# Two zero columns between prompt and sample tokens, and a pool of its own for the split-y ring, in a four-layer diffusion backbone

## The chip, the cores and the metric

One core of one Trainium2 chip. The metric is the device time of one execution in microseconds. TensorE is called PE below, its weight loads PEld, VectorE DVE, ScalarE ACT, GpSimd POOL and SyncE SP. L340 is line 340 of the kernel before.

## The reference

One inference step of a hybrid backbone, in float32: 128 prompt tokens and 256 sample tokens, D = 1024, four layers. Layers 0 and 3 mix tokens with a bidirectional Mamba-2 scan (SSD), layer 1 with a short gated convolution, layer 2 with differential attention. Each layer is followed by an FFN with a depthwise convolution. Around every sub-layer stand an RMS norm, and a shift, a scale and a gate that are computed from the condition with `w_mod`.

```python
def dwconv(x, w):                      # per group: prompt and sample each padded with zeros
    out = xp[:, 0:L] * w[0]
    for i in range(1, k):              # k = 3
        out = out + xp[:, i:i + L] * w[i]

def conv_ffn(h, w_up, conv_w, w_down):
    u = dwconv(h @ w_up, conv_w)
    gate, val = jnp.split(u, 2, axis=-1)
    return (jax.nn.silu(gate) * val) @ w_down

def ssd_mixer(...):
    z, xbc, dt_raw = jnp.split(h @ w_in, ...)
    xbc = jax.nn.silu(dwconv(xbc, conv_w) + conv_b)
    ...                                # scan forwards and backwards in chunks of 128 tokens
    y = rmsnorm(y * jax.nn.silu(z), norm_g)
    return y @ w_out
```

## The kernel before, in words

All 384 tokens (one tile of 128 prompt tokens, two tiles of sample tokens) go through the layers together. The normed and modulated activations h lie channel-major: hh and hl, eight blocks of 128 channels by T = 384 tokens, are two float32r parts whose sum is h. Weights are loaded in chunks of 128x1024 (`ahead`, L143), split in two float32r parts on ACT (L155) and DVE (L156), four chunks ahead of their use.

**Channel-major products** (`cm_block`, L331): for each block of 128 output channels PE runs 8 x 3 matmuls (hi hh, hi hl, lo hh) of 128x384 into one PSUM bank (L340). The FFN has 44 such blocks in a layer, an SSD layer 6 in each of its 8 groups, the short convolution 24.

**Convolutions** (`conv`, L393): ACT copies the block out of PSUM times the middle tap (L396). DVE then adds the left and the right neighbour, for the prompt's 128 columns and the samples' 256 apart, since the two groups must not mix: four instructions of 127 and 255 columns (L398, L400). Their last one lets the PSUM bank go. The products have five banks in the FFN and three (mm) beside two (yp) in an SSD layer.

**The SSD layer** (`ssd` L508, `ssd_core` L611): a loop over 8 groups. The scan of group g (`scan`, L645) is written in five steps, between which the products of group g + 1 are written (L754 to L758). `decay(t)` (L674) builds the weights of a token tile on POOL (L678, L679), DVE (L682, L686, L687, L693) and ACT; `out(t)` (L717) multiplies them into the two yp banks (L722), three tiles side by side in 384 columns. L741 reads both banks to the end and writes y. `gated` (L634) multiplies with the gate (L637), squares on ACT (L642) and sums on POOL (L643). In the last group no further products are written beside the scan except the gate's.

Memory: y, ssq and the ring of split y (yh, yl, seven each, `prep` L528) belong to the pool `mix`, which is open for the whole layer. The pool `core` holds dt, nine slots c (convolved blocks and squares), acs, wdt and dec, and above it the pool `scan` holds ab, st, xt, cb and others. When they close, their memory goes to the pool `out` of the output stage. These pools have `reuse_waits="tile"`: a tile waits for the tiles that lay in its memory.

**The output stage** (`_tm_out`, L359): token-major products of 128x512, two halves, k outermost: nine matmuls for each k (L380), with `prep(k)` splitting y[k] on ACT (L532) and DVE (L533) at most three k ahead as written. In the FFN L405 and L406 do this for fg.

The order of the instructions on each engine is made by the framework's scheduler from a simulated timeline, not by the order as written: an instruction that is ready early can be placed early, and each engine then works in that fixed order. Modulation (L187, 1 MB of `w_mod` for each unit) is written between the products by `pace` (L242).

Of the kernel before, what the change touches and what calls it, by code (L numbers as in the profile page):

```python
# [19 lines left out]
P = 128  # L20
D = 1024
KB = D // P
T = 384
# [9 lines left out]
TOK = [(0, 128), (128, 128), (256, 128)]  # L33
# [11 lines left out]
class Net:  # L45
# [22 lines left out]
    @contextmanager  # L68
    def banked(self, **banks):
        """Five banks of PSUM, by what they are for."""  # L70
        with self.tc.tile_pool(name="ps", bufs=1, space=PSUM, reuse_waits="tile") as ps:
            self.ps, self.banks = ps, banks
            yield
# [46 lines left out]
    def plan(self, l):  # L120
        """The chunks of weights that layer l multiplies with, in their order."""
# [21 lines left out]
    def ahead(self):  # L143
        """Start the loads and the splits of the next chunks."""
# [22 lines left out]
    def mod_units(self, l):  # L167
        """Closures that compute layer l's modulation; a unit is a megabyte of w_mod."""
# [56 lines left out]
    def modbuf(self):  # L225
        """A buffer for a unit of w_mod: the standing ones, or one of those that a phase has room for."""
# [15 lines left out]
    def pace(self, phase, n, of):  # L242
        """Modulation beside the products of a phase, n parts of which are done."""
# [22 lines left out]
    def rstd(self, sa, sb, eps=EPS):  # L266
        """(sa + sb + eps) ** -0.5"""
# [11 lines left out]
    def normed(self, t, ss):  # L279
        """The rows of token tile t, normed."""  # L280
# [7 lines left out]
    def turned(self, xn, banks=0):  # L288
        """Channel-major: two banks of [128 channels, 4 blocks, 128 tokens]."""
# [8 lines left out]
    def modulated(self, l, which, t, trs):  # L298
        """h's columns of token tile t, in two float32r parts."""
# [14 lines left out]
    def gated(self, t, hf, acc, gt, parts):  # L314
        """Half a token tile of m: its squares' sum and its product with the gate."""
# [5 lines left out]
    def residual(self, t, parts, eps=EPS):  # L321
        """x += gate * rmsnorm(m) * g for token tile t; the new rows' sums of squares."""
# [8 lines left out]
    def cm_block(self, chunks, nblk, b, m=P, tag="mm"):  # L331
        """[m channels, tokens] of h @ W; chunks: (first kb, number, hi, lo) as [128, kb, nblk, m]."""
# [18 lines left out]
    def tm_out(self, *args, room, **kw):  # L351
        """m = g @ W token-major, both halves, then the residual of each token tile."""
# [40 lines left out]
    def conv(self, src, cw):  # L393
        """Depthwise convolution of three taps along the tokens of both groups."""
        t = self.cpool.tile([P, T], F32, tag="c", name="cv", bufs=self.cbufs)
        self.S.activation(t, src, AF.Copy, scale=cw[:, 1:2])  # L396
        for o, n in ((0, 128), (128, 256)):
            self.V.scalar_tensor_tensor(t[:, o + 1:o + n], src[:, o:o + n - 1], cw[:, 0:1], t[:, o + 1:o + n],  # L398
                                        op0=ALU.mult, op1=ALU.add)
            self.V.scalar_tensor_tensor(t[:, o:o + n - 1], src[:, o + 1:o + n], cw[:, 2:3], t[:, o:o + n - 1],  # L400
                                        op0=ALU.mult, op1=ALU.add)
# [7 lines left out]
    def run(self):  # L409
# [24 lines left out]
        for n, l in enumerate(self.layers):  # L434
# [4 lines left out]
            def norm(t, ss, l, which):  # L439
                if t == 0:  # L440
                    self.new_h()
# [66 lines left out]
    def ssd(self, l, pl, then):  # L508
# [11 lines left out]
        # eps over the square of the rows' norm factor, which is left out of y  # L520
        sp = self.pt.tile([P, 512], F32, tag="tp", name="sps")
        for t in range(NT):
            PE.matmul(sp[:, t:t + 1], ssq[:, t * P:(t + 1) * P], self.ones1, start=True, stop=True)
# [4 lines left out]
        def prep(k):  # L528
            hi = pl.tile([P, T], F32R, tag="yh", name="yh", bufs=RB)
            lo = pl.tile([P, T], F32R, tag="yl", name="yl", bufs=RB)  # L530
            g = dn[:, k // 2, k % 2, 1:2]
            S.activation(hi, y[k], AF.Copy, scale=g)  # L532
            V.scalar_tensor_tensor(lo, y[k], g, hi.bitcast(F32), op0=ALU.mult, op1=ALU.subtract)  # L533
            return hi, lo

        self.tm_out(l, 0, 16, prep, eps=eps, then=then, room=1)

    def steps(self, j, keep, pl, between):
        """Time steps and decays: dt, the cumulated a*dt (token-major, and by rows in DRAM), and what states need."""
# [10 lines left out]
        for t in range(NT):  # L550
            PE.transpose(tr[:, t, :64], raw[:, t * P:(t + 1) * P], self.ident[:64, :64])
# [8 lines left out]
        # log1p(u) = 2 atanh(z), z = u / (2 + u) <= 1/3  # L560
# [17 lines left out]
        # cumulated within a chunk, forwards and backwards: rows of heads  # L578
        rows = pl.tile([64, T], F32, name="rows")
# [440 lines left out]
```

## Time and profile before

| | |
|---|---|
| median of 3 runs | 2426.16 us (2422.03 to 2428.34) |
| the profiled execution: span of core 0 | 2425.7 us (no time of its own outside the span is listed) |
| instructions | 35610 |
| mean granted clock of PE | 0.974 of 2.4 GHz |
| PE, DVE, ACT, POOL busy | 2298.7, 1647.8, 1225.8, 378.5 us |

Stages of the span: SSD layer 0 from about 60 to 455 us (scan groups up to 380), its FFN to 755; the short convolution to 870, with its output stage and norms to 925, its FFN to 1200; attention to 1460, its FFN to 1755; SSD layer 3 to 2140 (groups up to 2071), its FFN to the end. Busy times of PE count a matmul from its start to its modelled end, and matmuls overlap, so the start-to-start time of neighbours is the pace, not the duration of one.

### The profile page before, as it was taken

What the parts mean: (1) busy time and instruction counts of PE and PEld (TensorE: products, weight loads), DVE (VectorE), ACT (ScalarE), POOL (GpSimd) and SP (SyncE); (2) the same over time, 40 slices, a digit from 0 to 9 for tenths busy, and PEclk for the clock granted to TensorE, in tenths of its full rate; (3) what the DMA queues carried; (4) which work ended last, traced back from release to release, by engine and by line L of the source; (5) the groups of instructions that cost most, each with busy time, mean ns of one, the idle gap of its engine ahead of it and who ended that gap; (6) DMA issues with size and microseconds to landing.
All of it is one profiled execution on the core that took longest, in us unless ns stands there. A gap on an engine that the chain in (4) does not pass through costs nothing.

```text
span 2425.7 us, 35610 instructions
## 1 busy us (share of the span) xinstructions
PE 2298.7 (95%) x13132; PEld 2007.5 (83%) x13132; DVE 1647.8 (68%) x2926; ACT 1225.8 (51%) x2031; POOL 378.5 (16%) x546
## 2 busy tenths in 40 slices
PE   6889999899999999999999989999998999989998
PEld 3778887599987978998688758998687888779987
DVE  3789877487755447776654547776669988677765
ACT  3646656454444344444544444445555766554444
POOL 1133330100001001000123330000114344010000
PEclk7989999999999999999999989999999999989999
DMA  7556565543547564335435453345455655423342
GB/s 285 173 164 194 171 202 191 200 137 122 165 120 268 212 215 162 130 122 165 148 116 178 164 205 128 123 131 163 138 171 174 194 160 162 133 97 122 126 146 85
DMA packets 113374, 391.79 MB, mean 162 GB/s; under 512 B 13104, under 2 KB 25520, under 8 KB 100912
## 3 DMA queue, kind: packets, MB, share of 16 engines
q1 hardware_dynamic: 113200, 389.52, 49.1%
q8 instruction: 103, 1.69, 0.3%
q14 instruction: 71, 0.58, 0.1%
HBM read 382.39 MB, written 7.08 MB: 161 GB/s over the span
## 4 chain that ended last, share of the span: by engine, by line
PE 76%; DVE 8%; DMA 3%; issue 2%; ACT 2%; POOL 2%; SPq 0%; POOLq 0%; DVEq 0%; ACTq 0%
PE mm L340 42%; PE mm L380 20%; PE mm L807 5%; PE modps L187 2%; PE yp L380 2%; DVE w L686 2%; DVE e L682 1%; DVE wl L156 1%; PE yp L848 1%; PE yp L722 1%; DMA wm<-in_w_mod 1%; DMA h<-in_state 1%; ACT jk L263 1%; DVE w L687 1%; POOL r L273 1%
## 5 line engine op out<-in xcount | busy, mean ns | idle before, releaser
L340 PE MATMUL mm<-hh,wh 128*128 128x384 f32 (+1 forms) x2352 | 798.0, 341 | 19.1 <-DVE cv L400 13.6
L340 PE MATMUL mm<-hl,wh 128*128 128x384 f32 (+1 forms) x2352 | 796.1, 339 | 0.0
L340 PE MATMUL mm<-hh,wl 128*128 128x384 f32 (+1 forms) x2352 | 792.1, 338 | 0.0
L156 DVE TENSOR_TENSOR wl<-wr,wh 128x1024 fp32r<-128x1024 f32 (+2 forms) x466 | 565.3, 1215 | 262.9 <-ACT wh L155 261.1
L155 ACT ACTIVATE wh<-wr 128x1024 fp32r<-128x1024 f32 (+2 forms) x466 | 483.2, 1039 | 328.0 <-PE mm L340 265.0
L340 PEld LDWEIGHTS mm<-hh,wh 128*128 128x128 f32 (+1 forms) x2352 | 444.3, 189 | 45.6 <-DVE cv L400 20.4
L340 PEld LDWEIGHTS mm<-hl,wh 128*128 128x128 f32 (+1 forms) x2352 | 443.9, 189 | 6.5 <-issue 4.2
L340 PEld LDWEIGHTS mm<-hh,wl 128*128 128x128 f32 (+1 forms) x2352 | 443.6, 189 | 2.6 <-issue 0.7
L396 ACT ACTIVATE cv<-mm,fcw 128x384 f32<-128x384 f32 x176 | 100.1, 571 | 233.2 <-PE mm L340 228.2
L380 PE MATMUL mm<-wh,gh 128*128 128x512 f32 x528 | 208.7, 395 | 0.0
L380 PE MATMUL mm<-wl,gh 128*128 128x512 f32 x528 | 208.6, 395 | 0.0
L380 PE MATMUL mm<-wh,gl 128*128 128x512 f32 x528 | 207.9, 395 | 0.0
L271 POOL TENSOR_SCALAR m<-s 128x1 f32<-128x1 f32 x42 | 17.6, 419 | 1146.7 <-ACT jk L263 1145.8
L398 DVE SCALAR_TENSOR_TENSOR cv<-mm,fcw,cv 128x127 f32<-128x127 f32 x352 | 144.1, 410 | 42.6 <-ACT cv L396 42.6
L405 ACT ACTIVATE gh<-fg 128x384 fp32r<-128x384 f32 x176 | 92.2, 524 | 152.6 <-PE mm L380 151.7
L406 DVE TENSOR_TENSOR gl<-fg,gh 128x384 fp32r<-128x384 f32 x176 | 97.6, 557 | 96.7 <-ACT gh L405 96.0
L400 DVE SCALAR_TENSOR_TENSOR cv<-mm,fcw,cv 128x127 f32<-128x127 f32 x352 | 145.8, 415 | 10.8
L380 PEld LDWEIGHTS mm<-wh,gh 128*128 128x128 f32 x528 | 99.0, 187 | 24.9 <-issue 0.8
L380 PEld LDWEIGHTS mm<-wh,gl 128*128 128x128 f32 x528 | 99.0, 187 | 24.3
L380 PEld LDWEIGHTS mm<-wl,gh 128*128 128x128 f32 x528 | 99.0, 187 | 23.9
L686 DVE SCALAR_TENSOR_TENSOR w<-cb,dt,w 128x128 f32<-128x128 f32 x192 | 94.8, 550 | 3.2 <-POOL w L679 3.2
L187 PE MATMUL modps<-wm,sil 128*32 128x512 f32 x496 | 81.8, 658 | 14.1 <-DMA wm<-in_w_mod 13.2
(223 smaller groups left out, 3206.2 us busy)
## 6 DMA issues: line engine op xcount, KB each, us to landing
wr<-in_ffn_up SPq DMA_DIRECT2D x176, 512.0 KB
wm<-in_w_mod SPq DMA_DIRECT2D x62, 1024.0 KB
wr<-in_ssd_in SPq DMA_DIRECT2D x96, 512.0 KB
wr<-in_ffn_down SPq DMA_DIRECT2D x88, 512.0 KB
wx<-in_w_mod SPq DMA_DIRECT2D x34, 1024.0 KB
ab<-acs SPq DMA_DIRECT2D x48, 512.0 KB
wr<-in_ssd_out SPq DMA_DIRECT2D x32, 512.0 KB
wr<-in_sc_in SPq DMA_DIRECT2D x32, 384.0 KB
```

Source lines behind the costliest of these rows:

```text
L155: self.S.activation(hi[:, :m], raw[:, :m], AF.Copy)
L156: self.V.tensor_tensor(lo[:, :m], raw[:, :m], hi[:, :m].bitcast(F32), op=ALU.subtract)
L187: self.PE.matmul(acc[32 * j:32 * j + 32, :], self.sil[:, kb, :], raws[:, j // 2, (j % 2) * 512:(j % 2 + 1) * 512], start=kb == 0, stop=kb ...
L340: self.PE.matmul(acc[:m], w, h, start=n == 0, stop=n == len(ops) - 1)
L380: self.PE.matmul(acc[t], g[:, o:o + n], w, start=k == 0 and i == 0, stop=k == nk - 1 and i == 2)
L396: self.S.activation(t, src, AF.Copy, scale=cw[:, 1:2])
L398: self.V.scalar_tensor_tensor(t[:, o + 1:o + n], src[:, o:o + n - 1], cw[:, 0:1], t[:, o + 1:o + n], op0=ALU.mult, op1=ALU.add)
L400: self.V.scalar_tensor_tensor(t[:, o:o + n - 1], src[:, o + 1:o + n], cw[:, 2:3], t[:, o:o + n - 1], op0=ALU.mult, op1=ALU.add)
L405: self.S.activation(hi, src, AF.Copy)
L406: self.V.tensor_sub(lo, src, hi.bitcast(F32))
L686: V.scalar_tensor_tensor(w[:, sl], cb[:, 0, t, :], dt[:, t, hs:hs + 1], w[:, sl], op0=ALU.mult, op1=ALU.add)
L807: PE.matmul(acc[t][:, :256], h[k][:, o:o + m], w[:, ws], start=k == 0 and i == 0, stop=k == KB - 1 and i == 2)
```

## The change

h gets two zero columns between prompt and samples: T is 386, and the token tiles lie at 0, 130 and 258. hh and hl are made once, their gap is set to zero once, and later layers write the three tiles again; `norm` no longer makes new ones. Every tile with T columns is two columns wider, and every channel-major product yields zeros in the gap, so a convolution is two sums of 385 columns over the whole row. In the scan the gap of each yp bank is set to zero on DVE before L722 writes the tiles, as L741 reads all T columns. Slices `t * P:(t + 1) * P` of such tiles become `TS[t]`. The ring of split y moves from the pool `mix` to a pool `yhl`, opened after `core` has closed.

```diff
-T = 384
+GAP = 2
+T = 384 + GAP
-TOK = [(0, 128), (128, 128), (256, 128)]
+TOK = [(0, 128), (128 + GAP, 128), (256 + GAP, 128)]
+TS = [slice(o, o + m) for o, m in TOK]
...
     def new_h(self):
         hh = [self.hp.tile([P, 4, T], F32R, name=f"hh{i}") for i in range(2)]
         hl = [self.hp.tile([P, 4, T], F32R, name=f"hl{i}") for i in range(2)]
+        for a in hh + hl:
+            self.V.memset(a[:, :, P:P + GAP].bitcast(F32), 0.0)
...
     def conv(self, src, cw):
         t = self.cpool.tile([P, T], F32, tag="c", name="cv", bufs=self.cbufs)
         self.S.activation(t, src, AF.Copy, scale=cw[:, 1:2])
-        for o, n in ((0, 128), (128, 256)):
-            self.V.scalar_tensor_tensor(t[:, o + 1:o + n], src[:, o:o + n - 1], cw[:, 0:1], t[:, o + 1:o + n],
-                                        op0=ALU.mult, op1=ALU.add)
-            self.V.scalar_tensor_tensor(t[:, o:o + n - 1], src[:, o + 1:o + n], cw[:, 2:3], t[:, o:o + n - 1],
-                                        op0=ALU.mult, op1=ALU.add)
+        self.V.scalar_tensor_tensor(t[:, 1:], src[:, :T - 1], cw[:, 0:1], t[:, 1:], op0=ALU.mult, op1=ALU.add)
+        self.V.scalar_tensor_tensor(t[:, :T - 1], src[:, 1:], cw[:, 2:3], t[:, :T - 1], op0=ALU.mult, op1=ALU.add)
         return t
...
             def norm(t, ss, l, which):
-                if t == 0:
-                    self.new_h()
...
-        def prep(k):
-            hi = pl.tile([P, T], F32R, tag="yh", name="yh", bufs=RB)
-            lo = pl.tile([P, T], F32R, tag="yl", name="yl", bufs=RB)
...
-        self.tm_out(l, 0, 16, prep, eps=eps, then=then, room=1)
+        with self.tc.tile_pool(name=f"yhl{l}", bufs=1, reuse_waits="tile") as yp:
+            def prep(k):
+                hi = yp.tile([P, T], F32R, tag="yh", name="yh", bufs=RB)
+                lo = yp.tile([P, T], F32R, tag="yl", name="yl", bufs=RB)
...
+            self.tm_out(l, 0, 16, prep, eps=eps, then=then, room=1)
...
             mv1 = decay(1)
             yp = [self.psum("yp") for _ in range(2)]
+            for b in range(2):
+                V.memset(yp[b][:, P:P + GAP], 0.0)
             out(0, mv0)
```

## Rows read from the trace of the kernel before

**Rows 1.** The page, part 1: busy time of each engine.
```profile
PE 2298.7 (95%) x13132; PEld 2007.5 (83%) x13132; DVE 1647.8 (68%) x2926; ACT 1225.8 (51%) x2031; POOL 378.5 (16%) x546
```

**Rows 2.** Busy times by stage: window and its length, engines, granted clock, DMA share, GB/s.
```profile
125.00:367.00 242.00, 225.80 (x1471) 198.00 (x1472) 204.82 (x385) 146.47 (x206) 90.33 (x93) 0.96 0.58 183
...
925.00:1108.00 183.00, 183.00 (x1057) 182.92 (x1057) 134.35 (x248) 80.31 (x115) 0.00 (x0) 1.00 0.39 124
...
1850.00:2060.00 210.00, 204.09 (x1381) 185.36 (x1380) 189.79 (x359) 143.06 (x201) 88.25 (x85) 1.00 0.57 172
```
The five engines stand in the order PE, PEld, DVE, ACT, POOL.

**Rows 3.** Waits, whole run: us in total, times, longest us.
```profile
PE mm L340 <- DVE cv L400: 13.6, 14, 2.4
...
PE yp L722 <- DVE w L687: 13.4, 8, 4.6
```

**Rows 4.** The page's group of L340, and PE's timeline: start us, us, engine, line, operation.
```profile
L340 PE MATMUL mm<-hh,wh 128*128 128x384 f32 (+1 forms) x2352 | 798.0, 341 | 19.1 <-DVE cv L400 13.6
...
362.59 0.39 PE L380 MATMUL mm<-wl,yh 128*128 128x512 f32 x1
...
364.93 0.40 PE L380 MATMUL mm<-wh,yl 128*128 128x512 f32 x1
...
559.84 0.33 PE L340 MATMUL mm<-hh,wh 128*128 128x384 f32 x1
...
562.96 0.33 PE L340 MATMUL mm<-hh,wh 128*128 128x384 f32 x1
```

**Rows 5.** Timeline of DVE in the scan core of layer 3, at 1998.
```profile
1997.89 0.34 DVE L400 SCALAR_TENSOR_TENSOR cv<-mm,cw,cv 128x127 f32<-128x127 f32 x1
1998.15 0.47 DVE L398 SCALAR_TENSOR_TENSOR cv<-mm,cw,cv 128x255 f32<-128x255 f32 x1
1998.55 0.33 DVE L682 SCALAR_TENSOR_TENSOR e<-ab,acs,e 128x128 f32<-128x128 f32 x1
```

**Rows 6.** Groups by line, DVE, each form apart: a memset.
```profile
L103 DVE MEMSET ones<- 128x1 f32 x1 | 0.1, 59 | 0.0
```

**Rows 7.** ACT's busy time on L532 alone, windows in layers 0 and 3.
```profile
125.00:350.00 225.00, 4.23 (x7) 0.96 0.58 185
1830.00:1940.00 110.00, 4.23 (x7) 0.98 0.64 190
```

**Rows 8.** Timeline of DVE and POOL, end of the scan in layers 0 and 3.
```profile
377.79 1.13 DVE L741 SCALAR_TENSOR_TENSOR y<-cv,dn,yp 128x384 f32<-128x384 f32 x2
...
2069.88 1.13 DVE L741 SCALAR_TENSOR_TENSOR y<-cv,dn,yp 128x384 f32<-128x384 f32 x2
...
380.02 3.26 POOL L643 TENSOR_TENSOR ssq<-ssq,sq 128x384 f32<-128x384 f32 x2 [12.29 <-ACT sq L642]
...
2072.11 2.54 POOL L643 TENSOR_TENSOR ssq<-ssq,sq 128x384 f32<-128x384 f32 x2 [10.19 <-ACT sq L642]
```

**Rows 9.** PE and PEld on L380 alone, from the tail's start to four moments.
```profile
355.00:376.90 21.90, 9.60 (x38) 6.87 (x39) 1.00 0.46 157
355.00:382.00 27.00, 14.70 (x59) 10.98 (x60) 1.00 0.53 181
2050.00:2068.90 18.90, 11.91 (x44) 7.99 (x45) 1.00 0.27 73
2050.00:2073.00 23.00, 16.01 (x61) 11.31 (x62) 1.00 0.36 102
```

**Rows 10.** DVE on L533 alone, in both tails, up to L741.
```profile
355.00:377.70 22.70, 2.36 (x4) 1.00 0.47 157
2050.00:2069.80 19.80, 2.35 (x4) 1.00 0.28 76
```

**Rows 11.** Busy times and granted clock at the turn of layer 3, columns as in rows 2.
```profile
2130.00:2150.00 20.00, 11.55 (x53) 10.51 (x54) 13.12 (x23) 10.53 (x26) 5.79 (x8) 0.66 0.20 68
```

**Rows 12.** Timeline of DVE: end of decay(0) and of decay(1) in one group.
```profile
1985.25 0.68 DVE L687 TENSOR_TENSOR w<-w,e 128x512 f32<-128x512 f32 x1
...
1990.22 0.68 DVE L687 TENSOR_TENSOR w<-w,e 128x512 f32<-128x512 f32 x1
```

More of the change, by code (lines that the diff above doesn't have):

```diff
@@ L522, in ssd @@
         for t in range(NT):
-            PE.matmul(sp[:, t:t + 1], ssq[:, t * P:(t + 1) * P], self.ones1, start=True, stop=True)
+            PE.matmul(sp[:, t:t + 1], ssq[:, TS[t]], self.ones1, start=True, stop=True)
         ep = pl.tile([P, NT], F32, name="ep")
@@ L526, in ssd @@
         eps = [ep[:, t:t + 1] for t in range(NT)]
-        def prep(k):
-            hi = pl.tile([P, T], F32R, tag="yh", name="yh", bufs=RB)
-            lo = pl.tile([P, T], F32R, tag="yl", name="yl", bufs=RB)
[L531 to L534, printed above, removed]
-        self.tm_out(l, 0, 16, prep, eps=eps, then=then, room=1)
+        with self.tc.tile_pool(name=f"yhl{l}", bufs=1, reuse_waits="tile") as yp:
+            def prep(k):
+                hi = yp.tile([P, T], F32R, tag="yh", name="yh", bufs=RB)
+                lo = yp.tile([P, T], F32R, tag="yl", name="yl", bufs=RB)
+                g = dn[:, k // 2, k % 2, 1:2]
+                S.activation(hi, y[k], AF.Copy, scale=g)
+                V.scalar_tensor_tensor(lo, y[k], g, hi.bitcast(F32), op0=ALU.mult, op1=ALU.subtract)
+                return hi, lo
+            self.tm_out(l, 0, 16, prep, eps=eps, then=then, room=1)
     def steps(self, j, keep, pl, between):
@@ L550, in steps @@
         for t in range(NT):
-            PE.transpose(tr[:, t, :64], raw[:, t * P:(t + 1) * P], self.ident[:64, :64])
+            PE.transpose(tr[:, t, :64], raw[:, TS[t]], self.ident[:64, :64])
         dt = keep.tile([P, NT, 64], F32, name="dt")
@@ L577, in steps @@
         between()
-        rows = pl.tile([64, T], F32, name="rows")
+        rows = pl.tile([64, NT * P], F32, name="rows")
         for dr, tri in ((0, self.Ur), (1, self.Lr)):
@@ L584, in steps @@
                     PE.matmul(ps[:64, t * P:(t + 1) * P], a[:, t, :], tri, start=n == 0, stop=n == 1)
-            V.tensor_copy(rows[32 * dr:32 * dr + 32], ps[32 * dr:32 * dr + 32, :T])
+            V.tensor_copy(rows[32 * dr:32 * dr + 32], ps[32 * dr:32 * dr + 32, :NT * P])
         gd = self.dp.tile([NT, 2, 32, P], F32, name=f"acs{j}")
@@ L662, in scan @@
                 for t in range(NT):
-                    PE.transpose(tr[:, t, :], src[:, t * P:(t + 1) * P], self.ident)
+                    PE.transpose(tr[:, t, :], src[:, TS[t]], self.ident)
                 S.activation(dst, tr[:, 0:3, :], AF.Copy)
@@ L666, in scan @@
             for t in range(NT):
-                PE.matmul(cbp[:, t, :], Bc[:, t * P:(t + 1) * P], Cc[:, t * P:(t + 1) * P], start=True, stop=True)
+                PE.matmul(cbp[:, t, :], Bc[:, TS[t]], Cc[:, TS[t]], start=True, stop=True)
             cb = pl.tile([P, 2, NT, P], F32, tag="cb", name="cb")
@@ L692, in decay @@
                     c3 = ce.rearrange("p r (h q) -> p (r h) q", h=4)
-                    V.tensor_tensor(c3, c3, Cc[:, None, t * P:(t + 1) * P].to_broadcast([P, 8, P]), op=ALU.mult)
+                    V.tensor_tensor(c3, c3, Cc[:, None, TS[t]].to_broadcast([P, 8, P]), op=ALU.mult)
                     mv += [(hst[t, dr], ce[:, dr]) for dr in range(2)]
@@ L721, in out @@
                             hh = 2 * b + i
-                            PE.matmul(yp[b][64 * i:64 * i + 64, t * P:(t + 1) * P], a[:, hh * HP:(hh + 1) * HP],
+                            PE.matmul(yp[b][64 * i:64 * i + 64, TS[t]], a[:, hh * HP:(hh + 1) * HP],
                                       m[:, hh * P:(hh + 1) * P], start=n == 0, stop=n == len(mv) - 1, tile_position=(0, 64 * i))
@@ L789, in proj @@
         def proj(n, out):
-            qT = pl.tile([P, 2, T], F32, tag="qT", name="qT", bufs=2)
+            qT = pl.tile([P, 2, NT * P], F32, tag="qT", name="qT", bufs=2)
             kT = pl.tile([P, 2, 4 * P], F32, tag="kT", name="kT", bufs=2)
@@ L882, in heads @@
                     PE.transpose(tr[:, dh, :], on[:, dh, :], self.ident)
-                hi, lo = [a[n][:, :, t * P:(t + 1) * P] for a in (oh, ol)]
+                hi, lo = [a[n][:, :, TS[t]] for a in (oh, ol)]
                 S.activation(hi, tr[:, 0:2, :], AF.Copy, scale=gs)
```

## The prediction

> **What bounds the kernel now.** I read the page first: TensorE (PE) is busy 95% of the 2425.7 us span [rows 1]. Then the busy times by stage. In an FFN's up-projection (925 to 1108) PE is busy all of 183 us, while VectorE (DVE) has a quarter of its time to spare. In the scan cores of the two SSD layers (125 to 367, 1850 to 2060) DVE is busy 85% and 90%, and PE, with gaps, 93% and 97% [rows 2]. So a DVE instruction saved under an FFN buys nothing, one saved in an SSD core may. The table of waits gives the ceiling for that: in the whole run PE waited 13.6 us for a convolution to release its PSUM bank (L340 behind L400) and 13.4 us for the scan's weights (L722 behind L687) [rows 3], 27.0 us together.
>
> The queries by line and the timeline then settle the two prices that pull the other way: the pitch of the products, and what the ring of split y does today.
>
> **Two more columns in every channel-major product.** 3 x 2352 matmuls on L340 get 386 columns in place of 384. Their rows show 340 ns each, but they overlap: starts 18 apart lie 3.12 us apart, 173.3 ns per product, and 512-column products on L380 start 2.34 us apart for 10, 234 ns [rows 4]. (234 - 173.3) / 128 = 0.474 ns a column, 0.95 ns a product, 7056 x 0.95 = **6.7 us**, and nothing covers it, since PE is the engine that ends these stages. Bounds: nothing, if the granularity of the engine swallows two columns; 12.5 us, if the 340 ns of a row scaled (340 x 2 / 384 x 7056). I take 6.7, from the nearest widths.
> The Trainium skill (TensorE: Matmul & The Clock Gate, Back-to-back issue gap) has N / 2.4 + 2.5 ns for products back to back at full clock. By it two columns are 0.83 ns, 5.9 us in all; its level, 162.5 ns at 384 columns, is not what the trace shows (173.3), and the sum keeps the trace's slope.
>
> **Convolutions in two pieces.** Today each of 248 (176 FFN, 64 SSD, 8 short) issues four instructions on DVE. Rows of 340 and 474 ns overlap too: from the start of a 127-column piece to the next start it is 0.26 us, for a 255-column piece 0.40 us [rows 5]. That is 0.14 / 128 = 1.1 ns a column over a fixed 0.12 us, so 385 columns take 0.40 + 0.14 = 0.54 us. Four pieces: 2 x (0.26 + 0.40) = 1.32 us; two: 1.08 us; 0.24 us saved. In the FFNs and the short convolution (184 x 0.24 = 44 us) PE covers all of it: worth nothing, and its cover is PE at 100%. In the SSD layers 64 x 0.24 = 15.4 us leave DVE.
>
> Two other things change DVE's load there. The ring's first splits leave the core (below): 14 L533 of 384 columns, by the same rows 0.54 us each, 7.6 us. And 32 memsets of PSUM come in, one per yp bank and group; the only short memsets seen write 128x1 of SBUF in 59 ns [rows 6], and the fixed part of a piece is 0.12 us, so 1.9 to 3.8 us. DVE ends some 20 us lighter over both cores. PE's 27.0 us of waits bound the gain; below they bound it at nothing, because an instruction order made anew may put other DVE work in front of the same releases. I take **8 us**: half of the 13.6 us behind L400, where two pieces in place of four let the bank go, and about 1 us of the 13.4, of which 4.6 us is a single start-up wait that no convolution feeds.
>
> The other edits cost nothing: no DMA is added or dropped on SP's queue; the four memsets at the start run while the first weights land; a tile of h that is written again in place of a new one has the same readers, long done; two columns more on ScalarE's (ACT) and DVE's elementwise work lie beside PE.
>
> **The ring in its own pool.** This is the large term. prep makes (yh, yl) for the output product out of y[k], seven deep. Today the ring belongs to the mixer's pool and has memory that nothing else uses, so its first seven splits run far ahead: seven L532 between 125 and 350, seven between 1830 and 1940 [rows 7]. That is why PE has L380 work by 362.59 [rows 4], while the last group's scan, a chain on DVE without other products beside it, only ends with L741 at 377.79 (in the last layer 2069.88) [rows 8]. L380 fills that hole: 38 products until 376.9 and 59 until 382.0 in layer 0, 44 until 2068.9 and 61 until 2073.0 in layer 3 [rows 9].
> After the change the ring's pool opens when the core's pool has closed, and takes its memory. Tile by tile it waits for what lay there: dt first (read to the end by L686), then nine slots of the c ring, of which the last group's X0 and X1 hold two until L741, and its two squares two until L643 on POOL. The first pair (yh, yl) covers dt and three of the nine slots. With four of nine late, three drawn slots miss all four with 5 x 4 x 3 / (9 x 8 x 7) = 12%, and miss the squares with 7 x 6 x 5 / (9 x 8 x 7) = 42%. So the start of L380 moves to behind L741 or L643. Behind DVE's queue the tail itself is shorter: four L533 that stood in it [rows 10] come later, 4 x 0.54 = 2.2 us.
> - Held by L741: 377.79 - 2.2 + 0.6 (its own time) + 0.6 (the split on ACT, 4.23 / 7 [rows 7]) = 376.8, and 2068.9 in layer 3. Lost on PE: (38 + 44) x 0.234 = 19.2 us.
> - Held by L643: 380.02 + 3.26 - 2.2 + 0.6 = 381.7, and 2073.1. Lost: (59 + 61) x 0.234 = 28.1 us.
> - Below: 0, if the memory is free by 362. Above: without the 2.2 us of relief in each layer, 28.1 + 4.4 = 32.5 us.
> L643 is the likelier (58% against 30%), so I take **25 us**, nearer to it. The added wait is on ACT, in front of the first L532; behind it in ACT's queue stand the splits of the next weights (L155), then L156 and L533 on DVE and L380 on PE, which waits for the pair itself. The weights have four chunks in hand, so only the pair counts. What is late next: nothing, as one k costs PE nine products, 2.1 us, and ACT and DVE a little over half of that each. The pool for the output stage moves up by the ring's size, so its load of w_mod waits for other tiles; PE's later waits there are for norms, so no cost.
>
> **The clock.** A hole on PE has a second price. In the 20 us from 2130, with PE busy 11.55, the granted clock is 0.66 [rows 11]: 2 x 0.34 x 20 = 13.6 us at 1.2 GHz, of which 8.45 us were idle anyway, so 5.15 us of work ran at half rate and lost 2.6 us. The tails of the scan will have bursts (L704, L722) in their holes: 0 to 5.2 us for both, I take **2 us**.
>
> **The sum**: 6.7 + 25 + 2 - 8 = 25.7 us on 2425.7, **2451 us**. The execution of the page has no other time than its span; the median of the runs shown, 2426.16, is 0.5 us above it, within their spread.
>
> **The rivals.** A measurement of this kernel can tell 0.3%, 7.3 us, from no change.
> - *The ring is not held* (18%). Place: the first ring tile of each SSD layer. It decides if the split of y[0] is on ACT before the last group's final DVE work, that is if L380 again starts near 362 and 2053. Then 6.7 - 8 on 2425.7 gives **2424**, not slower. For it: five of nine slots are early, and a slot order that I can't see in the profile could hand the first tiles those. Against: three slots and dt have to be early at once.
> - *The ring is not held and DVE's relief takes all that it can* (10%): 6.7 - 27.0 gives **2405**, faster. For it: DVE at 85 to 90% is near its limit in the cores. Against: PE was busy 97% in the second, so little was lost there.
> - *No relief* (8%): the two long pieces stand in front of the scan's instructions as the four did; ring 32.5, clock 5.2, columns 6.7: **2470**.
> - *The memsets hold the scan's products* (6%). They are written behind decay(1); if the first L722 of a group has to wait for them, it waits from decay(0)'s L687 to decay(1)'s, about 5 us in [rows 12] (1985.25 to 1990.22). Sixteen groups bound it at 80 us, **2530**, if nothing stood in; it decides once the 24 products that PE can do meanwhile (24 x 0.1733 = 4.2 us) come behind L722 in PE's order. Against: the bank is free 20 us before, so an order made by readiness puts the memsets early.
> The Trainium skill (PSUM — Partial Sum Buffer, Terms) says that no two engines may touch the same bank of the same partitions at once; by that rule memset and L722 have to be kept apart although their columns differ, which is this rival. No row of this trace shows such a pair.
>
> **How the numbers follow.** The forecast with the ring held and some relief has 58%: 2436 (columns 6.7, ring 19.2, 15.4 off for DVE, no clock) to 2463 (columns 6.7, ring 32.5, 2 off). The rivals have 18, 10, 8 and 6. The range 2419 to 2463 leaves out the second rival (10%), the fourth (6%) and about half of the third (4%). Faster by over 0.3% (below 2418.4): the second rival and a little of the first, 12%. Within 0.3%: the rest of the first, 17%. Slower: 71%.
>
> **What would show it.** In the profile after: L340 at 386 columns with starts 174.2 ns apart; 496 convolution pieces in place of 992, 0.54 us each where they follow on; the first L532 of each SSD layer not before the last group's L741 or L643; on PE, in both tails, waits of L380 for yh or yl and a granted clock below 1. Waits behind L400 halved. I am wrong if L532 still runs ahead of the tail, if L340's pitch moves by more than 2 ns, or if L722 waits for a memset.

## The result, and the profile after

The kernel after takes 2483.4 us (median of 4 runs, 2482.7 to 2485.4), the kernel before beside it on the same chip 2424.1 us: a ratio of 1.0241, 95% interval 1.0226 to 1.0255. It is 59 us slower. The sign was forecast, the size was not: 2451 with a range to 2463. The profiled execution spans 2480.9 us, 55.2 more than that of before (2425.7), and the ledgers below are made of these two and of the profiled executions of the runs.

The page of after, part 1, answers to [rows 1]:

```profile
PE 2347.2 (95%) x13132; PEld 2040.3 (82%) x13132; DVE 1574.1 (63%) x2466; ACT 1225.5 (49%) x2029; POOL 369.6 (15%) x546
```

DVE did lose its work: 73.7 us and 460 instructions. PE has the same 13132 matmuls and is busy 48.5 us longer.

**The products.** The costliest group by line, and then PE's timeline in an FFN, 18 products apart as in [rows 4]:

```profile
L345 PE MATMUL mm<-hh,wh 128*128 128x386 f32 (+1 forms) x2352 | 810.7, 347 | 6.8 <-DVE hh L316 4.8 <-DVE cv L403 2.0
```

```profile
559.75 0.34 PE L345 MATMUL mm<-hl,wh 128*128 128x386 f32 x1
...
562.95 0.34 PE L345 MATMUL mm<-hl,wh 128*128 128x386 f32 x1
```

3.20 us for 18 is 177.8 ns, against 173.3. Over longer stretches of the FFNs the starts lie 177.2 ns apart, not as evenly as before: 3.9 ns a product where 0.95 was forecast.

**The ring.** The end of layer 3's scan in the timeline, four engines in order of time, answers to [rows 8]; a bracket holds the idle time before an instruction and what ended it:

```profile
2103.17 1.14 DVE L744 SCALAR_TENSOR_TENSOR y<-cv,dn,yp 128x386 f32<-128x386 f32 x2 [0.94 <-PE yp L723]
2105.42 2.07 POOL L644 TENSOR_TENSOR ssq<-ssq,sq 128x386 f32<-128x386 f32 x2 [11.68 <-ACT sq L643]
2105.72 0.60 ACT L533 ACTIVATE yh<-y,dn 128x386 fp32r<-128x386 f32 x1
2107.53 3.16 ACT L533 ACTIVATE yh<-y,dn 128x386 fp32r<-128x386 f32 x6 [1.21 <-POOL ssq L644]
2107.53 0.62 DVE L534 SCALAR_TENSOR_TENSOR yl<-y,dn,yh 128x386 fp32r<-128x386 f32 x1 [2.28 <-POOL ssq L644]
2107.55 1.44 PE L523 MATMUL sps<-ones,ssq 128*128 128x1 f32 x6 [4.21 <-POOL ssq L644]
2108.85 0.77 PE L385 MATMUL mm<-wh,yh 128*128 128x512 f32 x1
2109.42 0.63 PE L385 MATMUL mm<-wl,yh 128*128 128x512 f32 x1
...
2109.85 0.63 PE L385 MATMUL mm<-wh,yh 128*128 128x512 f32 x1
```

The first split of y follows the last L744, and the second hi and the first lo wait for the last L644 on POOL: the likelier branch of the forecast. PE's first output products (L385) come behind it; in PE's own order the row sums of ssq (L523), which need the same L644, stand ahead of them too. Their neighbours start 0.43 us apart (2109.42, then 2109.85) where [rows 4] have 0.234: PE works at the lower of its two clocks, 1.2 GHz, as the granted clock of that stretch says (the 0.50 here, columns as in [rows 2]):

```profile
2109.00:2112.00 3.00, 3.00 (x8) 2.32 (x9) 2.97 (x7) 1.89 (x5) 0.00 (x0) 0.50 0.00 0
```

In layer 0 the splits start as late (this is the view by line of L533):

```profile
L533 ACT ACTIVATE yh<-y,dn x16: 600/618/624, 373.7 to 399.1; 128x386 fp32r<-128x386 f32 x16
```

Windows over the two tails, up to the first output product (columns as in [rows 2]):

```profile
350.00:376.70 26.70, 17.26 (x130) 11.87 (x129) 22.17 (x39) 12.06 (x20) 9.64 (x11) 0.84 0.58 202
2080.00:2108.80 28.80, 17.51 (x117) 13.28 (x116) 23.10 (x41) 12.21 (x21) 12.21 (x13) 0.82 0.35 115
```

PE is busy 17.3 of 26.7 us at a granted clock of 0.84, and 17.5 of 28.8 at 0.82; before, these holes held 38 to 61 output products [rows 9].

**The waits** of the whole run, as in [rows 3]:

```profile
PE yp L723 <- DVE w L688: 25.4, 10, 5.7
...
PE mm L345 <- DVE cv L403: 2.0, 1, 2.0
```

What PE no longer waits for the convolutions (13.6 to 2.0) it waits for the scan's weights (13.4 to 25.4): 27.0 us before, 27.4 after. The longest of the latter, 5.5 and 5.7 us, stand in the tails that the output products used to fill.

**Stages.** I marked where the first product of each next stage starts on PE. The windows of the three stages that are not FFN or short convolution, after, and then before:

```profile
0.00:467.50 467.50, 412.55 (x2443) 334.06 (x2443) 328.13 (x567) 257.76 (x396) 126.53 (x146) 0.93 0.61 199
1228.30:1495.30 267.00, 247.12 (x1544) 184.78 (x1541) 125.10 (x257) 115.19 (x306) 74.05 (x181) 0.92 0.45 159
1791.90:2192.50 400.60, 368.55 (x2230) 322.91 (x2230) 310.83 (x536) 241.34 (x358) 122.83 (x131) 0.96 0.51 155
```

```profile
0.00:459.00 459.00, 404.58 (x2434) 329.90 (x2434) 339.12 (x614) 259.95 (x398) 129.68 (x146) 0.94 0.60 199
1214.90:1464.30 249.40, 234.03 (x1545) 181.03 (x1541) 124.58 (x257) 114.74 (x305) 78.34 (x181) 0.97 0.49 171
1757.30:2142.20 384.90, 356.42 (x2231) 315.24 (x2231) 316.69 (x585) 241.71 (x360) 125.06 (x131) 0.98 0.54 161
```

SSD layer 0 is 8.5 us longer, SSD layer 3 15.7, the four FFNs and the short convolution together 13.4. The other 17.6 us went in attention, where PE has the same work (1545 and 1544 matmuls counted) at a clock of 0.92 instead of 0.97, and is busy 13.1 us longer with it. The change touches nothing there but the width of rows (h's and those of the heads' outputs). That is the largest of the four terms, and the forecast had none for it. Work also moved between stages: one unit of modulation, 8 products, ran in the first FFN before and runs in SSD layer 0 after.

### The profile page after: what moved, and what is told of

It is laid out like the page before. It is cut to its first block, busy times and chain, and to the rows that moved or that the text cites. A ratio compares the mean times of both kernels' runs of the same rounds, so it can differ in the third digit from the quotient of the medians.

```text
span 2480.9 us, 35120 instructions
## 1 busy us (share of the span) xinstructions
PE 2347.2 (95%) x13132; PEld 2040.3 (82%) x13132; DVE 1574.1 (63%) x2466; ACT 1225.5 (49%) x2029; POOL 369.6 (15%) x546
## 5 line engine op out<-in xcount | busy, mean ns | idle before, releaser
L345 PE MATMUL mm<-hh,wh 128*128 128x386 f32 (+1 forms) x2352 | 810.7, 347 | 6.8 <-DVE hh L316 4.8
L345 PE MATMUL mm<-hh,wl 128*128 128x386 f32 (+1 forms) x2352 | 805.5, 343 | 0.0
L345 PE MATMUL mm<-hl,wh 128*128 128x386 f32 (+1 forms) x2352 | 804.4, 343 | 0.0
L401 ACT ACTIVATE cv<-mm,fcw 128x386 f32<-128x386 f32 x176 | 101.4, 576 | 243.4 <-PE mm L345 243.4
L385 PE MATMUL mm<-wh,gh 128*128 128x512 f32 x528 | 208.4, 395 | 0.0
L385 PE MATMUL mm<-wl,gh 128*128 128x512 f32 x528 | 208.0, 394 | 0.0
L385 PE MATMUL mm<-wh,gl 128*128 128x512 f32 x528 | 207.9, 395 | 0.0
L407 ACT ACTIVATE gh<-fg 128x386 fp32r<-128x386 f32 x176 | 92.6, 526 | 150.7 <-PE mm L385 150.5
L402 DVE SCALAR_TENSOR_TENSOR cv<-mm,fcw,cv 128x385 f32<-128x385 f32 x176 | 108.5, 616 | 83.3 <-ACT cv L401 83.3
L408 DVE TENSOR_TENSOR gl<-fg,gh 128x386 fp32r<-128x386 f32 x176 | 98.1, 559 | 97.2 <-ACT gh L407 96.6
L385 PEld LDWEIGHTS mm<-wh,gh 128*128 128x128 f32 x528 | 99.2, 188 | 24.6 <-issue 1.7
L385 PEld LDWEIGHTS mm<-wh,gl 128*128 128x128 f32 x528 | 99.1, 188 | 24.3 <-issue 0.8
L385 PEld LDWEIGHTS mm<-wl,gh 128*128 128x128 f32 x528 | 99.2, 188 | 23.5
L403 DVE SCALAR_TENSOR_TENSOR cv<-mm,fcw,cv 128x385 f32<-128x385 f32 x176 | 108.9, 619 | 5.2
L687 DVE SCALAR_TENSOR_TENSOR w<-cb,dt,w 128x128 f32<-128x128 f32 x192 | 99.9, 576 | 8.9 <-POOL w L680 8.9
```

The costliest lines, as they stand in the source:

```text
L345: self.PE.matmul(acc[:m], w, h, start=n == 0, stop=n == len(ops) - 1)
L385: self.PE.matmul(acc[t], g[:, o:o + n], w, start=k == 0 and i == 0, stop=k == nk - 1 and i == 2)
L402: self.V.scalar_tensor_tensor(t[:, 1:], src[:, :T - 1], cw[:, 0:1], t[:, 1:], op0=ALU.mult, op1=ALU.add)
L403: self.V.scalar_tensor_tensor(t[:, :T - 1], src[:, 1:], cw[:, 2:3], t[:, :T - 1], op0=ALU.mult, op1=ALU.add)
L407: self.S.activation(hi, src, AF.Copy)
L408: self.V.tensor_sub(lo, src, hi.bitcast(F32))
```

## The experiments

The same marks in every profiled execution give this ledger. us against the kernel before; the last column compares medians of runs, with the interval of the ratio. A sum comes from one execution of each kernel and differs from the medians by up to 7 us; the four engines of before_rows386 work in the same order as those of before, and its attention is still 4.2 us longer, so a stage's entry is not exact to less than that.

| kernel | SSD 0 | FFNs, short | attention | SSD 3 | sum | runs |
|---|---|---|---|---|---|---|
| after | +8.5 | +13.4 | +17.6 | +15.7 | +55.2 | 1.0241 (1.0226 to 1.0255) |
| before_rows386 | -0.8 | +7.2 | +4.2 | -1.0 | +9.6 | 1.0032 (1.0016 to 1.0049) |
| after_rows400 | +12.5 | +16.5 | +17.1 | +15.7 | +61.8 | 1.0250 (1.0227 to 1.0272) |
| ring_alone | +9.3 | -2.2 | +13.1 | +22.9 | +43.1 | 1.0199 (1.0182 to 1.0216) |
| ring_layer3 | -1.7 | -1.5 | +0.6 | +21.9 | +19.3 | 1.0108 (1.0080 to 1.0137) |
| columns_alone | +2.5 | +14.3 | +0.4 | -0.8 | +16.4 | 1.0086 (1.0059 to 1.0112) |
| after_ring_back | +1.9 | +13.8 | +8.5 | +1.7 | +25.9 | 1.0136 (1.0104 to 1.0169) |
| conv2_alone | +3.2 | -2.9 | +14.0 | +1.2 | +15.5 | 1.0081 (1.0054 to 1.0108) |
| conv2_rep1 | +2.5 | -1.0 | +2.6 | +3.8 | +7.9 | 1.0034 (1.0022 to 1.0046) |
| after_rep0 | +12.6 | +16.6 | +17.3 | +15.6 | +62.1 | 1.0257 (1.0241 to 1.0272) |
| after_rep1 | +10.3 | +14.5 | -1.4 | +16.4 | +39.8 | 1.0178 (1.0157 to 1.0198) |

### The price of two columns: place of the rows, or their number?

**micro**: the products by themselves, in 12 blocks of 144 (the list names tile, columns and row pitch).

```diff
+CFG = [("ha", 384, 384), ("hb", 386, 386), ("hc", 384, 386), ("hd", 386, 400), ...]
+                for q, (w, m) in enumerate(ops):
+                    nc.tensor.matmul(acc, w, m, start=q == 0, stop=q == len(ops) - 1)
```

> Leaves out the whole network; it only runs blocks of 24 float32r products (hi hh, hi hl, lo hh with eight k) on tiles of one name for each shape, six blocks each; its outputs carry no result. Read off: start-to-start time of neighbours by tile. 'Place' theory: what costs is that rows of hh and hl start off a boundary (386 columns are 1544 bytes). 'Count' theory: the engine works columns in steps of 8, and 386 cost what 392 do. 'Linear' (the prediction): 0.474 ns a column. ha (384 columns, rows 384 apart): 173.3 by all three. hb (386, rows 386 apart, the change): 177 by place and count, 174.2 linear. hc (384, rows 386 apart): place 177, count and linear 173.3. hd (386, rows 400 apart) and hi (386, rows 448 apart): place and linear 174.2, count 177. he (388, rows 400 apart): place 175.2, count 177. hf (392, rows 400 apart): 177.1 by all. hg (400): 180.9 by all. hj (382, rows 384 apart): count 173.3, others 172.4. hk (384, rows 388 apart, 1552 bytes): place 177 if the boundary is 32 bytes or more, else 173.3; count 173.3. The repeats of ha and hb at the end should agree with the first within 0.5 ns.

PE's timeline; the first product of a block to the first of the next, divided by 144, is the pace:

```profile
62.83 0.34 PE L946 MATMUL mm<-hc,wh 128*128 128x384 f32 x1
...
88.24 0.34 PE L946 MATMUL mm<-hd,wh 128*128 128x386 f32 x1
...
113.74 0.34 PE L946 MATMUL mm<-he,wh 128*128 128x388 f32 x1
...
267.56 0.34 PE L946 MATMUL mm<-ha,wh 128*128 128x384 f32 x1
...
292.52 0.34 PE L946 MATMUL mm<-hb,wh 128*128 128x386 f32 x1
```

ha (384 columns, rows 384 apart): 24.96 / 144 = 173.3 ns. hc (384 columns, rows 386 apart): 25.41 / 144 = 176.5. hd (386 columns, rows 400 apart): 25.50 / 144 = 177.1. By the same reading hb 176.1, he 177.2, hf (392) 177.7, hg (400) 182.2, hi (386, rows 448 apart) 176.7, hj (382) 179.9, hk (384, rows 388 apart) 174.4. (For ha this is its second stretch; the first, with a wait and 3.4 us at a granted clock of 0.51 in it, gave 221.0.) So place and number each cost about 3 ns, and not one on top of the other. Neither theory holds alone, the linear one not at all; hj shows that fewer columns can cost more.

**before_rows386** and **after_rows400** take the two halves into the kernels, with the order of instructions unchanged (the diff is the first's; hl the same, and 400 in the second):

```diff
-        hh = [self.hp.tile([P, 4, T], F32R, name=f"hh{i}") for i in range(2)]
+        hh = [self.hp.tile([P, 4, 386], F32R, name=f"hh{i}")[:, :, :T] for i in range(2)]
```

> The kernel before, 384 columns, with the rows of hh and hl 386 columns apart instead of 384; the order of instructions is the same. Place: L340's neighbours 177.5 ns apart, 7056 x 4.2 = 30 us more, less what the SSD cores' waits take up: 2445 to 2456. Count and linear: 173.3 ns, 2424 within 3.

> The kernel after with the rows of hh and hl 400 columns (1600 bytes) apart instead of 386, still 386 columns in a product; the order of instructions is the same. Place: pitch back to 174.2 ns, 7056 x 3.3 = 23 us less: about 2460. Count: pitch 177 to 178, 2483 within 3.

PE's timelines, 72 products apart, first before_rows386, then after_rows400:

```profile
1000.07 0.34 PE L340 MATMUL mm<-hl,wh 128*128 128x384 f32 x1
...
1012.69 0.34 PE L340 MATMUL mm<-hl,wh 128*128 128x384 f32 x1
```

```profile
1000.15 0.34 PE L345 MATMUL mm<-hh,wh 128*128 128x386 f32 x1
...
1012.91 0.34 PE L345 MATMUL mm<-hh,wh 128*128 128x386 f32 x1
```

12.62 / 72 = 175.3 ns with 384 columns in rows off their old place, and 12.76 / 72 = 177.2 with 386 columns in rows at a rounder one: the pace of after exactly. The place alone costs 2 ns and 8.8 us of the runs, between the two branches on record; with 386 columns rows 400 apart give nothing back (2485.3 us). So 386 columns cost what they cost in either place, and "place" alone doesn't explain the change.

**micro2** asked for the rule, with widths from 256 to 512.

```diff
+RUNS = [("hp", n) for n in (384, 256, 320, 352, 368, 376, 380, 382, 384, 386, 392, 400, 416, 448, 480, 512)] + ...
```

> Leaves out the whole network; blocks of 24 products as in the first such run, all rows 512 columns apart (then rows 384 apart), widths 256 to 512; its outputs carry no result. Theory 'line': neighbours start (512 width at 233.5, 384 at 173.3) on a line of 0.47 ns a column: 368 165.7, 376 169.5, 392 177.1, 400 180.9, 416 188.5, 448 203.6, 480 218.6. Theory 'even widths': 256, 384 and perhaps 512 run at an even pace and lie below the line of the others, which lie 2 to 7 ns above it on both sides: 376 and 380 not below 173, 382 near 180 in both rows.

```profile
193.37 0.34 PE L945 MATMUL mm<-hp,wh 128*128 128x384 f32 x1
...
218.34 0.34 PE L945 MATMUL mm<-hp,wh 128*128 128x386 f32 x1
...
243.77 0.34 PE L945 MATMUL mm<-hp,wh 128*128 128x392 f32 x1
...
269.30 0.52 PE L945 MATMUL mm<-hp,wh 128*128 128x400 f32 x2
...
295.22 0.35 PE L945 MATMUL mm<-hp,wh 128*128 128x416 f32 x1
```

384 columns: 24.97 / 144 = 173.4 ns; 386: 25.43 / 144 = 176.6; 392: 25.53 / 144 = 177.3; 400: 25.92 / 144 = 180.0. Read in the same way, 256, 320, 352, 368 and 512 give 119.9, 146.7, 160.0, 166.7 and 226.8, which with 384 and 400 is N / 2.4 + 13.3 ns. Between them it is uneven: 376 costs 173.3, as much as 384; 380 171.1; 416 188.3, 1.7 above that line. On that line 386 would be 174.1, next to the forecast's 174.2; it is 176.6, nearly what 392 cost. Neither theory on record holds: "line" has 169.5 for 376, "even widths" has 376 and 380 not below 173 and 382 near 180. No rule for the uneven ones came out of it. 382 columns in rows 384 apart gave 179.9 in the first run (hj) and 173.3 here, and 400 columns 182.2 (hg, rows 400 apart) and 180.0 (rows 512 apart), so columns alone don't set the pace; what does beside them stays open. What the change needs is settled: in every place tried 384 columns in rows 384 or 512 apart pace at 173.3 or 173.4, and 386 columns at 176.1 to 177.1.

**columns_alone** prices the columns in the kernel: gap, 386 columns and memsets, but four convolution pieces (around the gap) and the ring in its old pool (as in after_ring_back below, two small constants share a tile). The diff is against the kernel before.

```diff
-        for o, n in ((0, 128), (128, 256)):
+        for o, n in ((0, 128), (128 + GAP, 256)):
```

> 386 columns and the gap, but four convolution pieces as before and the ring in the mixer's pool. All of the pitch on the path: 2424 + 27.5 = 2452. With the SSD cores' waits taking up part, as the run with rows 386 apart showed (8.8 of 13.6 us): 2424 + 18 = 2442. Linear forecast of the columns: 2431.

2445.5 us, +20.4, nearest the branch with part of the pitch covered (2442): in the ledger 14.3 of 16.4 us stand in FFNs and the short convolution, 1.7 in the SSD layers. There are 4800 products in the former, 4800 x 3.9 = 18.7 us; the SSD layers' 2352 would be 9.2, of which most doesn't show in their length.

### The ring, and an attention stage that has none

**ring_alone**: the kernel before, with the pool `yhl` as in the change and nothing else.

```diff
+        with self.tc.tile_pool(name=f"yhl{l}", bufs=1, reuse_waits="tile") as yp:
...
+                hi = yp.tile([P, T], F32R, tag="yh", name="yh", bufs=RB)
```

> The kernel before with the ring of split y alone in a pool of its own. Ring held by L643 (forecast's likelier branch): first L380 of each tail behind the last L643, 28 us lost, clock 0 to 5: 2448 to 2460. Held by L741: 2443 to 2448. Not held: 2424 within 4, which would leave all of the change's loss to products and order.

2472.4 us, +48, above every branch. By the ledger the SSD layers pay 32.2 us, near the forecast's upper bound (32.5), and attention 13.1, in a kernel whose products, rows and convolutions are those of before. So the ring moves something that is not at the ring.

**ring_layer3** moves the ring in the last layer only, so that all that is scheduled ahead of it stays as it was.

```diff
+        yp = es.enter_context(self.tc.tile_pool(name=f"yhl{l}", bufs=1, reuse_waits="tile")) if l == 3 else pl
```

> The ring in a pool of its own in layer 3 alone; up to layer 3's core the order of instructions is that of before. Ring alone lost 48 us, by stages of its trace 9 in SSD layer 0, 13 in attention, which has no ring, and 23 in SSD layer 3. Theory 'order': attention's 13 us come from an order of instructions made anew behind layer 0, so here it is 249 us as before and only layer 3 pays: 2424 + 20 to 24 = 2444 to 2448. Theory 'tail only' (the forecast's price): 61 products x 0.234 = 14 us and 0 to 3 for the clock: 2438 to 2441. If attention is 13 us longer here too, the order is not its cause.

2451.3 us, +26.2, 3 us above the "order" branch; the profiled execution is the fastest of the four, 19.3 us longer than that of before. Windows of attention and of SSD layer 3:

```profile
1209.50:1459.50 250.00, 234.78 (x1545) 181.14 (x1541) 124.64 (x258) 114.80 (x305) 80.23 (x181) 0.96 0.49 170
1753.70:2160.50 406.80, 368.56 (x2231) 320.82 (x2231) 315.17 (x585) 239.53 (x356) 119.33 (x131) 0.96 0.52 152
```

Attention takes 250.0 us, as before (249.4). Layer 3 pays its 21.9 us alone, more than the 14 to 17 of the "tail only" price. So attention's loss comes from behind layer 0 by way of the order, or at least not by way of what the ring does in layer 3.

**after_ring_back** is the change without its ring (two small constants share a tile, since the ring was 32 bytes short of fitting).

```diff
-                hi = yp.tile([P, T], F32R, tag="yh", name="yh", bufs=RB)
+            hi = pl.tile([P, T], F32R, tag="yh", name="yh", bufs=RB)
```

> The kernel after with the ring of split y back in the mixer's pool (two small constants share a tile, so that it fits); columns, convolutions and memsets as in the change. Products at 386 columns measured 3.9 ns more: 7056 x 3.9 = 27.5 us. With the forecast's relief of 8: 2443. If the parts add up (59 - 48 = 11): 2435. If relief takes all of PE's waits: 2424. L380's first product runs before the tail again.

2456.8 us, +31.7, above all three numbers: the ring is worth 26.6 us of the change by runs (2483.4 - 2456.8), by the ledger 20.6 in the SSD layers and 9.1 in attention, and the convolutions, against columns_alone, another 11 the wrong way, of which attention has 8.1 (+8.5 against +0.4).

**conv2_alone** leaves only the two long pieces (and leaves out the border between prompt and samples).

```diff
-        for o, n in ((0, 128), (128, 256)):
-            self.V.scalar_tensor_tensor(t[:, o + 1:o + n], src[:, o:o + n - 1], cw[:, 0:1], t[:, o + 1:o + n],
...
+        self.V.scalar_tensor_tensor(t[:, 1:], src[:, :T - 1], cw[:, 0:1], t[:, 1:], op0=ALU.mult, op1=ALU.add)
...
```

> The kernel before, 384 columns, with two convolution pieces of 383 columns over the whole row; it leaves out the border between prompt and samples. Only the relief of DVE is left: forecast 8 us, 2416. None: 2424. All of PE's waits behind L400 and L687: 2397.

2444.3 us: 19 us slower, where three answers from no change to 27 us faster stood on record. Again attention has most of it, 14.0 us, in a stage without convolutions. The three parts of the change, each alone, add up to 43.1 + 16.4 + 15.5 = 75.0 us in the ledger, and the change has 55.2: they are not independent.

### The order of attention's instructions

In ring_alone, conv2_alone, after_ring_back, after_rows400 and after, one unit of modulation (8 matmuls in the trace) stands on PE ahead of a turn (a transposition) that it follows in before, before_rows386, columns_alone and ring_layer3: there are 56 modulation products ahead of the eleventh-last turn of a head's output in the first five, 48 in the others. It is a mark of the order and not all of it: of attention's 1540 matmuls some 180 stand in another order in after than in before. The first five take 257.9 to 267.0 us in attention, the others 249.4 to 253.6. conv2_alone, with 384 columns, has attention's instructions on all four engines in exactly the order of after, and takes 263.4. To test it the order has to change with nothing else: **after_rep1** and **after_rep0** are the kernel after with one DVE instruction issued twice, in front of layer 1's FFN, for token tile 1 or tile 0 (the diff is the first; the second has (1, 1, 0)).

```diff
-        self.V.tensor_scalar(n0, x0, r, None, op0=ALU.mult)
+        [self.V.tensor_scalar(n0, x0, r, None, op0=ALU.mult) for _ in range(2 if getattr(self, "cur", 0) == (1, 1, 1) else 1)]
...
```

> The kernel after with one instruction more: the norm's multiply of token tile 1 between layer 1's mixer and its FFN (L289, 128x512 on DVE, 0.5 us) is issued twice. It makes the scheduler place attention's instructions as in the kernel before (the fifth-last turn of a head's output stands behind 48 modulation products, not 56). Theory 'order' (the 17.6 us that attention lost come from the order alone): attention 249 to 254 us instead of 267, total 2483 - 13 to 18 = 2465 to 2470. If columns or the gap make attention slower: 2483 within 3.

> The control: the same multiply issued twice for token tile 0; attention's order stays that of the kernel after. Theory 'order': attention 267 us within 1, total 2483 within 4. If the doubled multiply itself helps: as the run with tile 1.

(The text of after_rep1 miscounts that turn as the fifth-last.) after_rep1 takes 2469.0 us and after_rep0 2486.3, as after. The whole of attention, and then two windows from 170 us behind its start, first after_rep0, then after_rep1, columns as in [rows 2]:

```profile
1235.50:1502.20 266.70, 247.18 (x1545) 184.95 (x1541) 125.37 (x258) 115.06 (x306) 74.09 (x181) 0.92 0.46 160
...
1405.50:1420.50 15.00, 12.78 (x66) 7.60 (x58) 4.72 (x14) 4.99 (x20) 4.39 (x15) 0.77 0.60 196
1420.50:1435.50 15.00, 13.19 (x28) 6.60 (x29) 7.63 (x17) 6.40 (x20) 5.48 (x17) 0.58 0.14 46
```

```profile
1230.40:1478.40 248.00, 229.81 (x1544) 178.29 (x1541) 123.75 (x257) 114.85 (x306) 78.07 (x181) 0.97 0.48 172
...
1400.40:1415.40 15.00, 12.70 (x69) 7.30 (x67) 8.25 (x23) 8.78 (x33) 7.17 (x23) 1.00 0.43 167
1415.40:1430.40 15.00, 14.45 (x62) 11.23 (x63) 4.85 (x12) 4.38 (x15) 4.53 (x14) 0.89 0.11 36
```

In the last window the one has 28 matmuls and the other 62, in about the same busy time: at a clock of 0.58 each lasts longer. Ahead of it PE's timeline of after_rep0 shows the turns of a head's output waiting, and no wait above 0.99 us in the other:

```profile
1407.25 0.30 PE L885 MATMUL tp<-ident,on 128*128 128x128 f32 x1 [0.36 <-DVE on L880]
1408.90 0.33 PE L885 MATMUL tp<-ident,on 128*128 128x128 f32 x1 [1.36 <-DVE on L880]
```

Attention is 248.0 us in after_rep1 and 266.7 in after_rep0. One more instruction made the kernel 17 us faster by runs. So the order is the cause of attention's loss; a part of columns and gap in it, if there is one, is no larger than the 4 us by which attention differs in one and the same order. How the order costs the time is in part a reading. PE is busy 17.4 of the 18.7 us longer, with the same matmuls at a clock of 0.92 instead of 0.97, and idle 19.5 and 18.2 us: the loss is in matmuls that last longer, not in waiting. What makes the clock fall in the one order is not shown: in the first of the two windows PE is idle for 2.2 us in after_rep0 and for 2.3 in after_rep1.

**conv2_rep1** gives the two long pieces the same order, by the same doubled multiply.

> Two convolution pieces of 383 columns in the kernel before (again without the border between prompt and samples), and the multiply of tile 1 issued twice, which gives attention the order of the kernel before. Theory 'order': of the 19 us that two pieces alone lost, 14 go: 2424 + 4 to 6 = 2428 to 2430. If the pieces themselves cost: 2444. If DVE's relief is worth what the forecast says once the order is equal: 2416.

2433.2 us, +8.4 (1.0034), 3 us above the branch of "order": 11 of the 19 us were order, and no relief appears. What is left stands in the SSD layers (+6.3 in the ledger). PE's waits, whole run:

```profile
PE mm L340 <- DVE cv L398: 13.0, 8, 5.5
```

Against [rows 3] the waits for convolutions fell from 14 to 8, but one of them now lasts 5.5 us. PE's and DVE's timeline around it:

```profile
293.13 0.60 DVE L397 SCALAR_TENSOR_TENSOR cv<-mm,cw,cv 128x383 f32<-128x383 f32 x1
293.66 1.12 DVE L683 SCALAR_TENSOR_TENSOR w<-cb,dt,w 128x128 f32<-128x128 f32 x4
294.71 0.60 DVE L397 SCALAR_TENSOR_TENSOR cv<-mm,cw,cv 128x383 f32<-128x383 f32 x1
295.24 1.21 DVE L690 TENSOR_TENSOR ab<-ab,cv 128x1024 f32<-128x1024 f32 x1
296.37 1.13 DVE L679 SCALAR_TENSOR_TENSOR e<-ab,acs,e 128x128 f32<-128x128 f32 x4
297.42 0.60 DVE L398 SCALAR_TENSOR_TENSOR cv<-mm,cw,cv 128x383 f32<-128x383 f32 x1
...
298.17 0.66 PE L340 MATMUL mm<-hh,wh 128*128 128x384 f32 x1 [5.51 <-DVE cv L398]
```

Between a bank's first piece (L397, the one at 293.13) and its last (L398), which lets it go, DVE's order has 3.8 us of other work: three groups of the scan's and the first piece of another bank. The fewer pieces save DVE time and the order spends it in front of the release. Whether another order would keep the relief wasn't tried.

## Why the forecast was right and wrong

The measured 55.2 us (by the profiled executions) are 29.5 more than the forecast's 25.7. Of these, 17.6 belong to a stage that the forecast priced at nothing, 6.7 to products, by what stands outside the SSD layers, and 5.2 to the SSD layers, where a relief was taken off that did not come.

- **The ring, 25 us: the mechanism right, the number partly luck.** It was held by the last L643 (now L644), as the likelier branch said, and the two SSD layers lost 8.5 + 15.7 = 24.2 us net. The pieces: from the end of the last square sum to the end of the last output product it was 443.4 - 383.3 = 60.1 and 2127.1 - 2074.7 = 52.4 us before, and is 453.0 - 375.5 = 77.5 and 2177.6 - 2107.5 = 70.1 after: 17.4 and 17.7 us, 35.1 together and above the forecast's upper bound (28.1 + 4.4 = 32.5). Before, 65 and 68 output products had started by then, 133 x 0.234 = 31.1 us; the clock below makes up the rest. The last square sum ends earlier in its turn: 7.8 us in layer 0, and counted from the start of SSD layer 3 (1757.3 and 1791.9) 317.4 - 315.6 = 1.8 there. The forecast had 4.4 for that, from splits that leave DVE's queue. So a price too low met a gain too low. The ring's share also depends on what stands around it: in the SSD layers it is 32.2 us alone (ring_alone) and 20.6 in the change (after against after_ring_back).
- **The clock, 2 us: small but low.** In layer 0 the first 11 output products take 4.84 us (376.84 to 381.68) in place of 11 x 0.234 = 2.57: 2.3 us. In layer 3 the first 9 take 3.77 us (2108.85 to 2112.62) in place of 2.11: 1.7. That is 4.0 us within the 35.1 above and within the forecast's bounds (0 to 5.2).
- **The columns, 6.7 us: the step failed.** It took 0.474 ns a column from 384 and 512, and what lies between them doesn't lie on a line: alone, 384, 386, 392 and 400 columns pace at 173.4, 176.6, 177.3 and 180.0 ns. The two columns cost 3.9 ns, not 0.95, and columns_alone 16.4 us in the trace and 20.4 in the runs. The bound of 12.5, a row's duration scaled, was no bound. (The 7056 also leave out 96 products into yp banks, 0.1 us at the forecast's price.) The pitch off by more than 2 ns, which the forecast named as a sign of being wrong, is the sign that came.
- **The relief, -8 us: the step failed.** The pieces came out as priced: the starts of L402 and of what follows it lie 0.53 us apart (287.79 to 288.32) against 0.54, 496 pieces in all. But with attention's order equal, two pieces alone bring the SSD layers +6.3 us (conv2_rep1), and on top of the columns 1.9 + 1.7 - (2.5 - 0.8) = +1.9 (after_ring_back), which is within what a stage differs by in one order. The sign that was named, waits behind L400 halved, came (13.6 to 2.0 us), but not from the pieces: with them alone the waits are 13.0 us. That relief is worth half of the waits behind L400 was an assumption about an order that would not stay. The rival "no relief" (8%, 2470) came nearer to the result than the forecast.
- **"The other edits cost nothing": the largest miss.** The forecast said that an instruction order made anew could eat the relief in the SSD cores. It did not see that the order is made anew from there to the end, in stages that the change doesn't touch. Attention: 17.6 us of the 55.2, brought back by one doubled instruction (248.0 against 266.7 us). That makes this the step that failed by most.
- **The memsets: no cost, as forecast.** 32 of them, and nobody waits for them in the view by line (in columns_alone PE did, twice, 1.6 us in all):

```profile
L736 DVE MEMSET yp<- x32: 60/60/60, 78.2 to 2079.6; 128x2 f32 x32
```

Added up, 24.2 (ring, clock and what the cores gained or lost) + 13.4 (columns in FFNs and short convolution, less a unit of modulation that moved out) + 17.6 (attention's order) = 55.2 us. The forecast had 25 + 2 - 8 = 19 for the first, 6.7 for all products and nothing for the third.

## What to carry to other kernels

Don't interpolate a matmul's pace between two round widths: two columns more on 384 cost four times their share here, and a tile padded for an elementwise engine's sake pays on the engine that is the bound. Where a scheduler makes the order of a whole program, an edit in layer 0 can move a stage behind it by more than its own effect; before a stage's loss is put down to the edit, look whether its order changed, and test it with an instruction that does nothing. An early ring of split operands that "uses memory that nothing else uses" is what fills the tail of a scan: price its memory by the work that would stand still without it. Here it was 32 bytes that did not fit, and two small constants in one tile made room for them (after_ring_back).

## What the runs showed of the hardware that was not expected

- In rows 512 apart (micro2) the pace of float32r products is N / 2.4 + 13.3 ns at 256, 320, 352, 368, 384, 400 and 512 columns, 0.7 to 3.4 ns above it at 376, 382, 386, 392, 416, 448 and 480, and 0.5 below it at 380. 384 columns in rows 386 apart pace at 176.5 ns alone and 175.3 in the kernel. The Trainium skill (TensorE: Matmul & The Clock Gate, Back-to-back issue gap) has N / 2.4 + 2.5 ns, which it calls the isolated gap of a single matmul; the slope over round widths agrees, the constant here is 13.3.
- Four decay pieces of 128x128 on DVE take 1.13 us at 296.37 in conv2_rep1 and 3.48 at 284.88, where POOL works beside them from 285.13 to 288.21. No run here took POOL's work away, so that one slows the other is not shown.
